# Experts in an order found on chip, and two matmul passes for the five smallest of them

## The chip, the cores and the metric

The kernel runs on one core of a Trainium2 chip. The metric is the time of one execution on the device in microseconds (us), taken as the median of several runs. One execution was also recorded by the hardware profiler; rows and traces below come from it. The engines are TensorE (PE, its weight loads PEld), VectorE (DVE), ScalarE (ACT), GpSimd (POOL) and SyncE (SP), which issues the transfers.

## The reference

A trunk of two layers on 256 tokens of 2048 channels, all f32. The first layer mixes (pooling and attention) and has a dense SwiGLU; the second mixes by spatial gating and has eight SwiGLU experts, of which each token uses two. Only the experts are touched:

```python
logits = jnp.dot(xt, w_router)                       # 256 x 8
top_vals, top_idx = lax.top_k(logits, 2)
top_w = jax.nn.softmax(top_vals, axis=-1)
gates = jnp.sum(one_hot(top_idx, 8) * top_w[..., None], axis=1)
for e in range(8):                                   # w_gu[e]: 2048 x 2816, w_down[e]: 1408 x 2048
    y = y + gates[:, e:e + 1] * swiglu(xt, w_gu[e], w_down[e])
h = layer_norm(alpha * h + y)
```

On the given inputs the router sends 42, 47, 57, 114, 53, 34, 109 and 56 tokens to experts 0 to 7.

## The kernel before

Every f32 operand of a large matmul is split in two parts: a rounded head and a remainder. A product takes three passes on TensorE: activation head by weight remainder, activation remainder by weight head, head by head (`mm3`, L115 to L119). A weight tile comes by one transfer into one of 5 `raw` buffers (L106), ScalarE casts the head `wh` from it (L107) and VectorE subtracts the remainder `wl` (L108); 4 buffers hold heads and 4 hold remainders. A tile has 4 chunks of 128 rows by 512 columns (1 MB) or less. The framework gives each engine its instructions in an order of its own, worked out ahead; an engine then works through its list in that order and waits on semaphores.

After the router, `top2` gives the choice of each token, and `pos1` gives each token its place, from 1 on, in each expert's list. An expert works on 128 slots. `gather` builds one-hot matrices (L819) that pick the tokens of two experts, multiplies the tokens' heads and remainders by them (L837, two experts side by side, 256 columns) and copies the result to SBUF as `xe` (L839). `slots` builds the transposed one-hot `DT` and the gate of each slot `gs`. `expert_up` does gate and up in three column blocks of 512, 512 and 384, each 16 chunks deep, and SwiGLU after each block (L527, L528, transposes L181, split L174 and L175). `expert_down` does four column blocks, 11 chunks deep; each ends in a scatter: head `yh` (L896) and remainder `yl` (L897) of the gated result, two matmuls by `DT` for each half of the tokens (L900, L901), and an add to `h` (L234). The experts run in the order 0 to 7. The pair's gather for experts 2 and 3 is done in steps within the down stage of expert 1, and so on. The first expert's first block is special: `lead` steps through gather, tokens' parts and loads.

After the last expert come the last LayerNorm (`final_norm`) and a test on the largest count, `most`: an If (L729) holds a loop that would handle tokens beyond 128 of an expert. The experts' loads all go through SP's queue, in order.

Of the kernel before, what the change touches and what calls it, by code (L numbers as in the profile page):

```python
# [10 lines left out]
F32 = mybir.dt.float32  # L11
F32R = mybir.dt.float32r
BF16 = mybir.dt.bfloat16
I32 = mybir.dt.int32
# [18 lines left out]
HALF = 2  # L33
RSQRT_MAGIC = float(0x5F3759DF)
# [7 lines left out]
C_MAIN = 520  # L42
# [7 lines left out]
def make_consts():  # L50
# [9 lines left out]
    c[:, C_IOTA8:C_IOTA8 + NEXP] = np.arange(NEXP)[None, :] - NEXP  # L60
    pos = np.arange(2 * P)
# [11 lines left out]
class Trunk:  # L73
# [23 lines left out]
    def load(self, src, w=CB):  # L97
# [8 lines left out]
        nc.sync.dma_start(raw, src)  # L106
# [532 lines left out]
    def moe(self, pm, stats, G, B):  # L639
# [3 lines left out]
        gall = pm.tile([P, 3, P], F32R, tag="gg", name="gg", bufs=1)  # L643
        nc.vector.tensor_copy(gall[:, 0, :], self.ident)
# [40 lines left out]
        gat = self.gather(xtok, [pos1[t][:, 0:2] for t in range(NT)], gg, 0, 0)  # L685
# [16 lines left out]
        first = lead()  # L702
        for t in range(NT):
            gv = gg[t][:, 1, :2 * NEXP].rearrange("p (e s) -> p e s", s=2)
            nc.scalar.copy(gv[:, :, 0], gates[t])
            nc.vector.tensor_tensor(gv[:, :, 1], gates[t], gv[:, :, 0].bitcast(F32), ALU.subtract)
# [100 lines left out]
    def gather(self, xtok, pos, gg, e, offset, num=2):  # L807
# [36 lines left out]
        def slots():  # L844
            for p in range(num):
                ps = self.ps()
                for t in range(NT):
                    mm(ps[:, t * 256:(t + 1) * 256], Dt[t][:, p, :], gg[t], start=t == 0, stop=True,
                       skip_group_check=True)
                DT = pm.tile([P, NT, P], F32R, tag="DT", name="DT", bufs=3)  # L850
                pv = ps.rearrange("p (a b) -> p a b", a=2)
                nc.scalar.copy(DT, pv[:, :, 0:P])
                gs = pm.tile([P, 1], F32, tag="gs", name="gs", bufs=4)
                nc.vector.tensor_reduce(gs, pv[:, :, P + 2 * (e + p):P + 2 * (e + p) + 2], AX.XY, ALU.add)
                DTs.append(DT)
                gss.append(gs)
        return xe, DTs, gss, quarter, slots

    def expert_up(self, e, gat, p, first=None):
        i, pm = self.i, self.pm  # L860
# [6 lines left out]
        for b, w in enumerate(EXP_W):  # L867
            accs = []
            for u in range(2):
# [4 lines left out]
                groups = self.loads(i["odd_moe_gu"][e, b * 2 + u] if b < 2 else i["odd_moe_gu2"][e, u], w)  # L874
                accs.append(self.block(groups, lhs, 0, w))
            hT.append(self.swiglu(pm, accs[0], accs[1], w, w // P, "m"))
        return hT

    def expert_down(self, e, gat, p, hT, first, stats, step=None):
# [3 lines left out]
        def lhs(k, t):  # L883
            return hT[k // 4][0][:, k % 4, :], hT[k // 4][1][:, k % 4, :]
        for n in range(NCB):
            if step is not None:
                step(n)
            groups = []
            for k in range(0, EXP_KC, PIECE):
                o, kc = k * CB * P, min(PIECE, EXP_KC - k)  # L890
                src = i["odd_moe_down"][e, n][o:o + kc * CB * P].rearrange("(p m) -> p m", p=P)
                groups.append(self.load(src))
            acc = self.block(groups, lhs, 0)
            yh = pm.tile([P, CB], F32R, tag="yh", name="yh", bufs=1)
            yl = pm.tile([P, CB], F32R, tag="yl", name="yl", bufs=1)
# [138 lines left out]
```

## Time and profile before

| what | us |
|---|---|
| runs of the kernel, median (lowest to highest) | 2174.91 (2174.14 to 2175.73) |
| profiled execution, its own time | 2175.96 |
| profiled execution, span of its instructions | 2174.2 |

The span is from the first to the last instruction in the trace; 1.8 us of the profiled time lie around it. Starts in the rows count from the start of the span.

### The profile page before, as it was taken

The page shows a single profiled execution, that of the slowest core. Times are in us where ns is not written, and L with a number is a line of the kernel's source. Part 1 is how long each engine was busy: PE and PEld are TensorE (multiplying, and loading weights), DVE is VectorE, ACT ScalarE, POOL GpSimd, SP SyncE. Part 2 cuts the span into 40 slices and gives each one's busy share as a digit, 9 for nine tenths or more (in the row PEclk, how much of TensorE's full clock was granted, in tenths as well). Part 3 has the DMA queues.
Part 4 walks back from the last instruction along what each step waited for, and adds up shares of the span by engine and source line. Part 5 has one row for each costly group of instructions (what it writes and reads, how often), then busy time and mean ns, then how long its engine had stood idle before and what let it go on. Part 6 is the DMA issues. An engine that isn't in the chain of part 4 may idle for free.

```text
span 2174.2 us, 24450 instructions
## 1 busy us (share of the span) xinstructions
PE 2140.0 (98%) x9955; PEld 1781.5 (82%) x9956; DVE 1456.7 (67%) x1225; ACT 1146.6 (53%) x962; POOL 1.6 (0%) x6
## 2 busy tenths in 40 slices
PE   9999999999999999999999999999999999999996
PEld 7888888888888888888788887888888888888884
DVE  5443566554454644556676546898889888888988
ACT  5444355343333433343644335766766767676764
POOL 0000000000000000000000000000000000000000
PEclk9999999999999999999999999999999999999998
DMA  8544645555454554545544643899989999998995
GB/s 347 217 147 145 233 180 208 211 194 191 157 215 172 213 189 169 204 169 218 213 182 166 235 155 117 320 352 357 340 331 367 347 336 342 346 352 322 371 351 213
DMA packets 82198, 537.80 MB, mean 247 GB/s; under 512 B 9504, under 2 KB 10656, under 8 KB 28192
## 3 DMA queue, kind: packets, MB, share of 16 engines
q1 hardware_dynamic: 82080, 536.18, 66.3%
q8 instruction: 80, 1.31, 0.2%
q14 instruction: 38, 0.31, 0.0%
HBM read 534.04 MB, written 2.10 MB: 247 GB/s over the span
## 4 chain that ended last, share of the span: by engine, by line
PE 93%; DVE 3%; ACT 2%; DMA 1%; issue 0%; SPq 0%; DVEq 0%; ACTq 0%
PE acc L118 29%; PE acc L119 28%; PE acc L117 28%; PE ps L181 2%; DVE wl L108 1%; PE ps L837 1%; ACT wh L107 1%; PE ps L900 1%; DMA raw<-in_odd_moe_down_dram 1%; DMA raw<-in_even_w_in_dram 1%; PE ps L901 1%; ACT lnT L259 0%; PE ps L575 0%; PE acc L135 0%; PE acc L629 0%
## 5 line engine op out<-in xcount | busy, mean ns | idle before, releaser
L108 DVE TENSOR_TENSOR wl<-raw,wh 128x2048 fp32r<-128x2048 f32 (+2 forms) x519 | 1121.3, 2178 | 391.5 <-ACT wh L107 390.8
L107 ACT CAST wh<-raw 128x2048 fp32r<-128x2048 f32 (+2 forms) x519 | 935.4, 1824 | 442.1 <-PE acc L119 399.3
L118 PE MATMUL acc<-wl,xh 128*128 128x512 f32 x928 | 363.3, 392 | 1.1 <-DVE wl L108 1.1
L117 PE MATMUL acc<-wh,xh 128*128 128x512 f32 x928 | 361.8, 390 | 0.1
L119 PE MATMUL acc<-wh,xl 128*128 128x512 f32 x928 | 361.6, 390 | 0.0
L118 PE MATMUL acc<-wl,xe 128*128 128x512 f32 (+1 forms) x752 | 280.7, 373 | 0.1
L119 PE MATMUL acc<-wh,xe 128*128 128x512 f32 (+1 forms) x752 | 279.4, 372 | 0.0
L117 PE MATMUL acc<-wh,xe 128*128 128x512 f32 (+1 forms) x752 | 278.6, 371 | 0.5 <-ACT wh L107 0.5
L118 PE MATMUL acc<-wl,hTh 128*128 128x512 f32 x704 | 277.3, 394 | 1.1 <-DVE wl L108 1.0
L119 PE MATMUL acc<-wh,hTl 128*128 128x512 f32 x704 | 276.1, 392 | 0.0
L117 PE MATMUL acc<-wh,hTh 128*128 128x512 f32 x704 | 274.8, 391 | 0.0
L118 PEld LDWEIGHTS acc<-wl,xh 128*128 128x128 f32 x928 | 174.4, 188 | 37.0 <-DVE wl L108 1.5
L117 PEld LDWEIGHTS acc<-wh,xh 128*128 128x128 f32 x928 | 174.2, 188 | 37.1 <-ACT xh L174 0.5
L119 PEld LDWEIGHTS acc<-wh,xl 128*128 128x128 f32 x928 | 174.4, 188 | 35.7 <-DVE xl L175 0.2
L118 PEld LDWEIGHTS acc<-wl,xe 128*128 128x128 f32 x752 | 141.2, 188 | 21.2 <-DVE wl L108 1.8
L117 PEld LDWEIGHTS acc<-wh,xe 128*128 128x128 f32 x752 | 141.2, 188 | 20.7 <-ACT wh L107 0.8
L118 PEld LDWEIGHTS acc<-wl,hTh 128*128 128x128 f32 x704 | 132.3, 188 | 30.3 <-DVE wl L108 3.5
L119 PEld LDWEIGHTS acc<-wh,xe 128*128 128x128 f32 x752 | 141.3, 188 | 19.0
L117 PEld LDWEIGHTS acc<-wh,hTh 128*128 128x128 f32 x704 | 132.3, 188 | 28.3
L119 PEld LDWEIGHTS acc<-wh,hTl 128*128 128x128 f32 x704 | 132.4, 188 | 26.4
L174 ACT CAST hTh<-ps 128x512 fp32r<-128x512 f32 (+1 forms) x46 | 26.2, 569 | 180.4 <-PE ps L181 180.4
L117 PE MATMUL acc<-wh,x0h 128*128 128x512 f32 x256 | 104.1, 409 | 2.5 <-ACT wh L107 2.5
(201 smaller groups left out, 1820.0 us busy)
## 6 DMA issues: line engine op xcount, KB each, us to landing
raw<-in_odd_moe_gu_dram SPq DMA_DIRECT2D x128, 1024.0 KB, 6.9
raw<-in_even_ffn_gu_dram SPq DMA_DIRECT2D x88, 1024.0 KB, 4.8
raw<-in_odd_moe_down_dram SPq DMA_DIRECT2D x64, 1024.0 KB, 7.0
raw<-in_odd_moe_gu_dram SPq DMA_DIRECT2D x64, 768.0 KB, 6.1
raw<-in_even_ffn_down_dram SPq DMA_DIRECT2D x44, 1024.0 KB, 4.8
raw<-in_odd_w_in_dram SPq DMA_DIRECT2D x32, 1024.0 KB, 4.8
raw<-in_even_w_in_dram SPq DMA_DIRECT2D x30, 1024.0 KB, 5.0
raw<-in_odd_moe_down_dram SPq DMA_DIRECT2D x32, 768.0 KB, 6.8
```

The costliest lines, as they stand in the source:

```text
L107: nc.scalar.copy(wh, raw)
L108: self.wl_ins = nc.vector.tensor_tensor(wl, raw, wh.bitcast(F32), ALU.subtract)
L117: mm(acc, xh, wh, start=first, stop=False)
L118: mm(acc, xh, wl, start=False, stop=False)
L119: mm(acc, xl, wh, start=False, stop=last)
L174: self.nc.scalar.copy(hi, src)
L181: self.nc.tensor.transpose(ps[:, j * P:(j + 1) * P], src[:, j * P:(j + 1) * P], self.ident)
L837: mm(o, xtok[t, c // 8][part][:, cs], Dt[t].rearrange("p a b -> p (a b)"), start=j == 0 and t == 0, stop=t == 1, skip_group_check=True)
L900: nc.tensor.matmul(ps, DT[:, t, :], yh, start=True, stop=False)
L901: nc.tensor.matmul(ps, DT[:, t, :], yl, start=False, stop=True)
```

## The change

An expert with at most 64 tokens needs only 64 slots. The change puts head and remainder of its 64 tokens side by side as the 128 columns of one stationary operand, so that a pass by `wh` and a pass by `wl` give all four products; the two halves of the result are then added by one more matmul by a shifted identity (`fold`) after a copy by ScalarE. Gate and up, and down, are done that way (`two`, `slim_expert`); in down the halves are added by the scatter's matmul, since the one-hots name each slot twice.

Which experts are that small is known only on chip. Expert 0 runs first, as before. During it `order` computes for the seven others a permutation: those with over 64 tokens first; SP reads the seven indices into registers, and the loads take their addresses from these. The first two in that order always run in three passes. For the last five an If on the number of experts over 64 (`full`) chooses: if it is at most two, the five run by `slim_expert`; else all run in three passes. Two loads of the first of the five are traced ahead of the If. The gathers are now of one expert (the first), of two, and within the If's first arm of two and of three; the arm's second gather is done in steps in the down stage of its second expert. The dispatch gates and positions are permuted by the same matrix. Loads, casts and remainders of the weights stay as they are. `down_loads`, `scatter` and `slots` hold lines that stood in `expert_down` and `gather` before.

```diff
+SLIM = 64
+EARLY = 2
+FATS = 2
+REST = NEXP - 1
...
-        nc.sync.dma_start(raw, src)
+        self.issued = nc.sync.dma_start(raw, src)
...
+        self.fold = pm.tile([P, P], F32R, tag="fold", name="fold", bufs=1)
+        nc.gpsimd.memset(self.fold[:, SLIM:].bitcast(F32), 0.0)
+        nc.gpsimd.tensor_copy(self.fold[:, :SLIM], self.ident[:, SLIM:])
...
-        gat = self.gather(xtok, [pos1[t][:, 0:2] for t in range(NT)], gg, 0, 0)
+        gat = self.gather(xtok, [pos1[t][:, 0:1] for t in range(NT)], gg, 0, 0, num=1)
...
+        def gate_cols(t, gates, at, num):
+            gv = gg[t][:, 1, at:at + 2 * num].rearrange("p (e s) -> p e s", s=2)
+            nc.scalar.copy(gv[:, :, 0], gates)
+            nc.vector.tensor_tensor(gv[:, :, 1], gates, gv[:, :, 0].bitcast(F32), ALU.subtract)
...
-        for e in range(NEXP):
-            cur = gat
-            hT = self.expert_up(e, cur, e % 2, None if e else first)
-            if e == 0:
+        many = pm.tile([P, REST], F32, tag="many", name="many", bufs=1)
+        nc.vector.tensor_scalar(many, cnt[:, 1:NEXP], float(SLIM), None, ALU.is_gt)
+        ids, posP, full = [], [], pm.tile([P, 1], I32, tag="full", name="full", bufs=1)
+
+        def gather(k, num):
+            return self.gather(xtok, [posP[t][:, k:k + num] for t in range(NT)], gg, NEXP + k, 0, num=num)
+
+        def gather_slim(k, num):
+            return self.gather_slim(xtok, [posP[t][:, k:k + num] for t in range(NT)], num)
+
+        def prepare():
+            order = self.order(many, pos1, gates, gate_cols, posP, full)
+            ins, v = nc.values_load_multi_w_load_instructions(
+                order[0:1, :], engines=[mybir.EngineType.SP], min_val=1, max_val=REST)
+            self.after(ins[0], self.issued)
+            ids.extend(v)
+        hT = self.expert_up(0, gat, 0, first, prepare)
+        gat[4]()
+        cur, gat = gat, gather(0, FATS)
+        gat[4]()
+        self.expert_down(0, cur, 0, hT, True, None, gat[3])
+        for p in range(FATS):
+            hT = self.expert_up(ids[p], gat, p)
+            self.expert_down(ids[p], gat, p, hT, False, None)
+        full_v = nc.values_load(full[0:1, 0:1], min_val=0, max_val=REST)
+        src = i["odd_moe_gu"][ids[FATS], 0]
+        early = [self.load(src[k]) for k in range(EARLY)]
+        with tc.If(full_v < FATS + 1) as slim:
+            at = 0
+            A, step = gather_slim(FATS, 2)
+            for q in range(4):
+                step(q)
+            for k in range(FATS, REST):
+                ahead = partial(gather_slim, k + 1, REST - k - 1) if k == FATS + 1 else None
+                nxt = self.slim_expert(ids[k], k - FATS - at, A, gg, NEXP + k, fstats if k == REST - 1 else None,
+                                       early if k == FATS else None, ahead)
+                if nxt is not None:
+                    A, at = nxt, 2
+        with slim.Else():
+            for k in range(FATS, REST, 2):
+                num = min(2, REST - k)
+                gat = gather(k, num)
                 gat[4]()
-            step = None
-            if e % 2 and e + 1 < NEXP:
-                gat = self.gather(xtok, [pos1[t][:, e + 1:e + 3] for t in range(NT)], gg, e + 1, 0)
-                gat[4]()
-                step = gat[3]
-            self.expert_down(e, cur, e % 2, hT, e == 0, fstats if e == NEXP - 1 else None, step)
+                for q in range(4):
+                    gat[3](q)
+                for p in range(num):
+                    hT = self.expert_up(ids[k + p], gat, p, early=None if k + p > FATS else early)
+                    self.expert_down(ids[k + p], gat, p, hT, False, fstats if k + p == REST - 1 else None)
 
...
+    def order(self, hv, pos1, gates, gate_cols, posP, full):
...
+        e7 = self.c[:, C_IOTA7:C_IOTA7 + R]
+        rank, a, b = (tile(f"ord{k}", [P, R]) for k in range(3))
+        H = tile("ordH", [P, 1])
+        ids = tile("ids", [P, R], I32)
+        sq, perm = tile("ordsq", [P, R, R]), tile("perm", [P, R, R])
+        self.after(v.tensor_reduce(H, hv, AX.X, ALU.add), self.wl_ins)
+        v.tensor_copy(full, H)
+        v.tensor_tensor(sq, rows(hv), square(C_LOWER), ALU.mult)
+        v.tensor_reduce(rank, sq, AX.X, ALU.add)
+        v.scalar_tensor_tensor(a, e7, H, rank, ALU.add, ALU.subtract)
+        v.tensor_tensor(b, rank, a, ALU.subtract)
+        v.tensor_tensor(b, b, hv, ALU.mult)
+        v.tensor_tensor(a, a, b, ALU.add)
+        v.tensor_tensor(perm, rows(a), square(C_PLACE), ALU.is_equal)
+        v.tensor_scalar(b, e7, 1.0, None, ALU.add)
+        v.tensor_tensor(sq, perm, rows(b), ALU.mult)
+        v.tensor_reduce(b, sq, AX.X, ALU.add)
+        v.tensor_copy(ids, b)
+        for t in range(NT):
+            g = tile("gateP", [P, R], bufs=2)
+            x = tile("posP", [P, R], bufs=2)
+            for dst, src in ((x, pos1[t]), (g, gates[t])):
+                v.tensor_tensor(sq, perm, rows(src[:, 1:NEXP]), ALU.mult)
+                v.tensor_reduce(dst, sq, AX.X, ALU.add)
+            gate_cols(t, g, 2 * NEXP, R)
+            posP.append(x)
+        return ids
...
+    def gather_slim(self, xtok, pos, num):
...
+        slots = self.iota1[:, :SLIM].unsqueeze(1).to_broadcast([P, 2, SLIM])
+        d4 = []
+        for t in range(NT):
+            d = pm.tile([P, num, 2, SLIM], F32R, tag="Dt", name="d4", bufs=2)
+            for p in range(num):
+                nc.vector.tensor_scalar(d[:, p], slots, pos[t][:, p:p + 1], None, ALU.is_equal)
...
+        A, units = {}, {}
+        per = 4 // num if num < 3 else 1
+        w = num * SLIM
+        hold = 8 // num if num < 3 else 2
+
+        def quarter(q):
+            for c in range(4 * q, 4 * q + 4, per):
+                if c % hold == 0:
+                    units[0] = self.unit("xs", shape=[P, hold, num, 2, SLIM])
+                ps = self.ps()
+                for j in range(per):
+                    cs = slice((c + j) % 8 * P, ((c + j) % 8 + 1) * P)
+                    for part in range(2):
+                        o = ps[:, (2 * j + part) * w:(2 * j + part + 1) * w]
+                        for t in range(NT):
+                            mm(o, xtok[t, (c + j) // 8][part][:, cs], d4[t][:, :, 0, :],
+                               start=j == 0 and part == 0 and t == 0, stop=t == 1, skip_group_check=True)
+                for j in range(per):
+                    u = units[0][:, (c + j) % hold]
+                    nc.scalar.copy(u, ps[:, 2 * j * w:2 * (j + 1) * w].rearrange("p (a e s) -> p e a s", a=2, e=num))
+                    A[c + j] = u
+        return (A, d4), quarter
...
+    def slim_expert(self, e, p, gat, gg, col, stats, early, ahead):
...
+        A, d4 = gat
+
+        def two(groups, lhs, w):
+            acc = self.acc()
+            n, k0 = sum(g[2] for g in groups), 0
+            for wh, wl, kc in groups:
+                for j in range(kc):
+                    mm(acc[:, :w], lhs(k0 + j), wh[:, j, :], start=k0 + j == 0, stop=False)
+                    mm(acc[:, :w], lhs(k0 + j), wl[:, j, :], start=False, stop=k0 + j == n - 1)
+                k0 += kc
+            return acc
+
+        def fold(acc, w):
+            c = self.pln.tile([P, CB], F32R, tag="lnT", name="low")
+            nc.scalar.copy(c[:, :w], acc[:, :w])
+            mm(acc[:, :w], self.fold, c[:, :w], start=False, stop=True, skip_group_check=True)
+
+        hT = []
+        for b, w in enumerate(EXP_W):
+            accs = [two(self.up_loads(e, b, u, early),
+                        lambda k: A[k][:, p], w) for u in range(2)]
+            for acc in accs:
+                fold(acc, w)
+            nch = w // P
+            s = self.pln.tile([P, CB], F32, tag="lnT", name="silu")
+            nc.scalar.activation(s[:, :w], accs[0][:, :w], AF.Silu)
+            nc.vector.tensor_tensor(s[:, :w], s[:, :w], accs[1][:, :w], ALU.mult)
+            pv = self.transpose4(s, nch)[:, :w].rearrange("p (c t) -> p c t", c=nch)[:, :, :SLIM]
+            h = pm.tile([P, 4, 2, SLIM], F32R, tag="hTh", name="hT2", bufs=3)
+            nc.scalar.copy(h[:, :nch, 0, :], pv)
+            nc.vector.tensor_tensor(h[:, :nch, 1, :], pv, h[:, :nch, 0, :].bitcast(F32), ALU.subtract)
+            hT.append(h)
+        DT, gs = self.slots([d4[t][:, p] for t in range(NT)], gg, col)
+        nxt, step = (None, None) if ahead is None else ahead()
+        for n in range(NCB):
+            if step is not None:
+                step(n)
+            acc = two(self.down_loads(e, n), lambda k: hT[k // 4][:, k % 4], CB)
+            self.scatter(acc, DT, gs, n, False, stats)
+        return nxt
...
+                accs.append(self.block(self.up_loads(e, b, u, early), lhs, 0, w))
             hT.append(self.swiglu(pm, accs[0], accs[1], w, w // P, "m"))
+            if then is not None and b == 0:
+                then()
...
```

## Rows read from the trace of the kernel before

**Rows 1.** The page's first part: busy us, share, instructions.

```profile
PE 2140.0 (98%) x9955; PEld 1781.5 (82%) x9956; DVE 1456.7 (67%) x1225; ACT 1146.6 (53%) x962; POOL 1.6 (0%) x6
```

**Rows 2.** Windows: us, busy PE, PEld, DVE, ACT, POOL (count), PEclk, DMA share, GB/s.

```profile
900.00:1000.00 100.00, 100.00 (x447) 82.38 (x446) 50.27 (x32) 39.92 (x26) 0.00 (x0) 1.00 0.47 173
1454.85:1559.06 104.21, 104.19 (x516) 89.26 (x515) 87.53 (x62) 77.43 (x66) 0.00 (x0) 1.00 0.93 348
1559.06:1654.54 95.48, 95.48 (x448) 81.45 (x447) 83.80 (x54) 65.38 (x46) 0.00 (x0) 1.00 0.92 345
2055.34:2152.68 97.34, 96.48 (x447) 80.85 (x445) 85.30 (x59) 63.34 (x45) 0.00 (x0) 1.00 0.87 330
1454.85:2152.68 697.83, 696.03 (x3333) 592.84 (x3331) 598.82 (x397) 492.54 (x375) 0.00 (x0) 1.00 0.92 344
```

**Rows 3.** Waits, 1400 to 2100: us in total, times, longest; then SP's queue.

```profile
ACT wh L107 <- PE acc L119: 36.8, 48, 1.3
...
DVE silu L528 <- PE acc L119: 19.4, 17, 2.0
...
ACT wh L107 <- DMA raw<-in_odd_moe_down_dram: 9.3, 12, 1.4
...
SPq L106 <- DVE wl L108: 595.0, 252, 5.2
```

**Rows 4.** Windows where the DMA share is 1.00, columns as in rows 2.

```profile
20.00:50.00 30.00, 29.79 (x131) 24.35 (x131) 16.84 (x11) 15.13 (x14) 0.00 (x0) 1.00 1.00 410
1368.00:1390.00 22.00, 22.00 (x100) 18.19 (x100) 20.65 (x12) 15.79 (x10) 0.00 (x0) 1.00 1.01 392
1430.00:1450.00 20.00, 20.00 (x89) 16.48 (x89) 19.59 (x15) 14.49 (x11) 0.00 (x0) 1.00 1.00 365
```

**Rows 5.** Groups by line and shape from 1340 on: busy us, mean ns.

```profile
L839 ACT CAST xe<-ps 128x512 fp32r<-128x512 f32 x64 | 34.7, 592 | 13.4 <-PE ps L837 13.3
...
L819 DVE TENSOR_SCALAR Dt<-c,pos 128x128 fp32r<-128x128 f32 x16 | 3.5, 282 | 0.0
```

**Rows 6.** Lines L728, L729: ns min/median/max, first and last start.

```profile
L728 SPq TENSOR_LOAD <-most x1: 472/472/472, 1347.6 to 1347.6; - x1
...
L728 SPq FUSED_REGOPS  x1: 179/179/179, 1348.1 to 1348.1; - x1
...
L729 PEldq COMPARE_BRANCH  x1: 3370/3370/3370, 2155.0 to 2155.0; - x1
...
L729 DVEq COMPARE_BRANCH  x1: 72/72/72, 2169.0 to 2169.0; - x1
```

**Rows 7.** Timelines by engine: start, us, instruction, idle before.

```profile
1343.52 0.16 DVE L789 TENSOR_REDUCE idx<-eq 128x1 f32<-128x8 f32 x1
...
1364.80 13.30 DVE L108 TENSOR_TENSOR wl<-raw,wh 128x2048 fp32r<-128x2048 f32 x6
...
1376.46 1.92 ACT L107 CAST wh<-raw 128x2048 fp32r<-128x2048 f32 x1 [0.80 <-PE acc L119]
...
1422.86 0.66 ACT L852 CAST DT<-ps 128x256 fp32r<-128x256 f32 x2
...
1306.54 1.06 PE L629 MATMUL acc<-gR,rT 128*128 128x8 f32 x8
...
1359.41 1.10 PE L837 MATMUL ps<-Dt,xth 128*128 128x256 f32 x8
```

**Rows 8.** The page's sixth part: issues, KB each, median us to landing.

```profile
raw<-in_odd_moe_gu_dram SPq DMA_DIRECT2D x128, 1024.0 KB, 6.9
```

**Rows 9.** Timelines of the tail, ScalarE, then VectorE.

```profile
2152.68 0.69 ACT L896 ACTIVATE yh<-acc,gs 128x512 fp32r<-128x512 f32 x1 [7.84 <-PE acc L119]
...
2154.74 1.28 DVE L234 TENSOR_TENSOR h<-h,ps 128x512 f32<-128x512 f32 x2 [0.59 <-PE ps L901]
```

**Rows 10.** TensorE's timeline and a window, columns as in rows 2.

```profile
1347.03 2.05 PE L837 MATMUL ps<-Dt,xth 128*128 128x256 f32 x8 [1.94 <-DVE Dt L819]
...
1345.20:1348.60 3.40, 1.57 (x7) 1.61 (x8) 3.40 (x17) 0.84 (x3) 0.00 (x0) 0.50 0.00 0
```

More of the change, by code (lines that the diff above doesn't have):

```diff
@@ L845, in slots @@
             for p in range(num):
[L846 to L854, printed above, removed]
+                DT, gs = self.slots([Dt[t][:, p, :] for t in range(NT)], gg, e + p)
                 DTs.append(DT)
@@ L857, in gather, with slots @@
         return xe, DTs, gss, quarter, slots
-    def expert_up(self, e, gat, p, first=None):
-        i, pm = self.i, self.pm
+    def slots(self, d, gg, col):
+        nc, pm = self.nc, self.pm
+        ps = self.ps()
+        for t in range(NT):
+            nc.tensor.matmul(ps[:, t * 256:(t + 1) * 256], d[t], gg[t], start=t == 0, stop=True,
+                             skip_group_check=True)
+        DT = pm.tile([P, NT, P], F32R, tag="DT", name="DT", bufs=3)
+        pv = ps.rearrange("p (a b) -> p a b", a=2)
+        nc.scalar.copy(DT, pv[:, :, 0:P])
+        gs = pm.tile([P, 1], F32, tag="gs", name="gs", bufs=4)
+        nc.vector.tensor_reduce(gs, pv[:, :, P + 2 * col:P + 2 * col + 2], AX.XY, ALU.add)
+        return DT, gs
@@ L861, in expert_up @@
+    def expert_up(self, e, gat, p, first=None, then=None, early=None):
+        pm = self.pm
         xe = gat[0]
@@ L887, in expert_down, with up_loads, down_loads, scatter @@
                 step(n)
[L888 to L895, printed above, removed]
-            nc.scalar.mul(yh, acc, gs)
-            nc.vector.scalar_tensor_tensor(yl, acc, gs, yh.bitcast(F32), ALU.mult, ALU.subtract)
-            for t in range(NT):
-                ps = self.ps()
-                nc.tensor.matmul(ps, DT[:, t, :], yh, start=True, stop=False)
-                nc.tensor.matmul(ps, DT[:, t, :], yl, start=False, stop=True)
-                self.add_stats(t, n, ps, None if stats is None else stats[t], first)
+            acc = self.block(self.down_loads(e, n), lhs, 0)
+            self.scatter(acc, DT, gs, n, first, stats)
+    def up_loads(self, e, b, u, early):
+        i = self.i
+        src = i["odd_moe_gu"][e, b * 2 + u] if b < 2 else i["odd_moe_gu2"][e, u]
+        if early is None or b or u:
+            return self.loads(src, EXP_W[b])
+        return early + [self.load(src[k]) for k in range(EARLY, src.shape[0])]
+    def down_loads(self, e, n):
+        groups = []
+        for k in range(0, EXP_KC, PIECE):
+            o, kc = k * CB * P, min(PIECE, EXP_KC - k)
+            src = self.i["odd_moe_down"][e, n][o:o + kc * CB * P].rearrange("(p m) -> p m", p=P)
+            groups.append(self.load(src))
+        return groups
+    def scatter(self, acc, DT, gs, n, first, stats):
+        nc, pm = self.nc, self.pm
+        yh = pm.tile([P, CB], F32R, tag="yh", name="yh", bufs=1)
+        yl = pm.tile([P, CB], F32R, tag="yl", name="yl", bufs=1)
+        nc.scalar.mul(yh, acc, gs)
+        nc.vector.scalar_tensor_tensor(yl, acc, gs, yh.bitcast(F32), ALU.mult, ALU.subtract)
+        for t in range(NT):
+            ps = self.ps()
+            nc.tensor.matmul(ps, DT[:, t, :], yh, start=True, stop=False)
+            nc.tensor.matmul(ps, DT[:, t, :], yl, start=False, stop=True)
+            self.add_stats(t, n, ps, None if stats is None else stats[t], first)
     def load_consts(self):
```

31 lines of the change are left out of this document (25 added, 6 removed).

## Prediction

> **What bounds the kernel now.** I read the busy shares first. TensorE is busy 98% of the span [rows 1], so its work counts first. The change touches the eight experts alone, so I went to the stretches between the start of the last `yh` (L896) of one expert and that of the next. Seven of them make 697.8 us, the experts 1 to 7. An expert without a gather in its stretch takes 95.5 us, one with the next pair's gather 104.2, and TensorE is busy all through both [rows 2]. Its work explains the length: the dense stretch of the FFN gives 447 matmuls in 100 us, 0.224 us for 512 columns [rows 2]; an expert has 324 of 512 columns and 96 of 384, with 16 more for the scatter, so 324 x 0.224 + 96 x 0.168 + 16 x 0.224 = 92.3 us and a few transposes.
>
> What is next behind TensorE? In the same 95.5 us VectorE is busy 83.8 us, mostly in the 36 remainders of L108, and the DMA engines' share is 0.92 [rows 2]. In the waits of the expert stage the casts (L107) wait for TensorE to give back a `wh` buffer for 36.8 us and for a transfer of the down weights 9.3 us, and the queue that issues loads waits 595 us for VectorE to free a `raw` buffer [rows 3]. So loads are held back by TensorE, through buffers, with two other resources close behind. That is the point of the whole forecast: what is taken off TensorE is worth only what these two let through.
>
> Bytes: an expert has 2048 x 2816 + 1408 x 2048 f32 weights, 34.6 MB in 36 loads, 0.961 MB a load. Where the DMA share is 1.00, the trace shows 410 GB/s early in the kernel, 392 while the first expert refills its buffers, and 365 where VectorE is busy 98% as well [rows 4]. A load at these rates takes 2.34, 2.45 and 2.63 us. VectorE needs 83.8 / 36 = 2.33 us per load if it never waits.
>
> **Which arm runs.** The reference's router sends 42, 47, 57, 114, 53, 34, 109 and 56 tokens to the experts. Two of the last seven exceed 64, so `full` is 2, the condition `full < 3` holds, the two fat ones come first and the five others take two passes.
>
> **The change, part by part.**
>
> *Two passes instead of three, five times.* Per expert 64 + 44 matmuls of 512 columns and 32 of 384 go: 108 x 0.224 + 32 x 0.168 = 29.6 us, 148 us in all. Added per expert: six folds, 1.3 us. TensorE needs some 68 us per slim expert with its share of the gathers; loads take 36 x 2.34 to 36 x 2.63, 84 to 95 us. So the arm runs at the pace of the loads. I take 2.5 us a load, between the 392 and the 365 row, because VectorE and the transfers are nearly level there and five `raw` buffers tie them together; bounds 2.34 and 2.63. The loads' casts and remainders themselves stay as they are. ScalarE gains six fold copies (0.6 us each by the like of L839 [rows 5]) and stays under 75 us.
>
> *Small things.* The constants grow by 54 KB (0.13 us at 410 GB/s), and GpSimd builds the fold matrix while it has nothing else: 0.
>
> *Dynamic addresses.* A few register operations more per load on SP; one bundle of them took 0.18 us [rows 6]. The 595 us of waiting on that queue hide it; without that cover it were 252 x 0.18 = 45 us.
>
> *Order on chip.* `order` is 27 small VectorE instructions, some 0.2 us apart by the like of L789 [rows 7], 5 us, behind the remainder of load 7. VectorE works without a pause until 1378.1 there; TensorE gave back load 4's buffer at 1376.4 [rows 7] and has three more loads of 12 x 0.224 = 2.7 us, until 1384.5; the next remainder comes at 1385.6 instead of 1380.6: +1 us. Then SP loads seven registers; one load took 0.47 us and 0.18 of checks [rows 6], so 0.7 to 4.6 us. Behind it on SP stand the loads of the first expert's second block, and TensorE waits for them; the buffers already filled cover 10 us. If the instruction stands ahead of load 8 and waits for `ids`, transfers stop about 7 us and the chain landing (6.9 us [rows 8]), cast, remainder leaves TensorE idle some 8 us. I take +1, bounds 0 and +8; the like load for `most` stood on SP at 1347.6, where its data was ready [rows 6], not at the end of the program.
>
> *Gathers.* The first becomes one of a single expert: 16 copies of 128x256 instead of 128x512, 0.33 for 0.59 us [rows 5, 7], 4.2 us of ScalarE, of which I count half since others overlap: -2 (0 to -4). TensorE gains nothing: 8 matmuls of 8 columns take 1.06 us, 8 of 256 take 1.10 [rows 7], so narrow ones cost the same; eight follow each other at some 0.117. The pair's gather moves into the first expert's down stage, +8.7 us as before (104.2 - 95.5). The gathers of two and three stand in the arm; the second is hidden, since TensorE has slack there.
>
> *Entry of the arm.* Nothing of the arm can run ahead of the branch. From the second fat expert's last matmul: `yh`, `yl`, scatter and two adds, 3.4 us by the tail [rows 9]; register load 0.5 and branch 0.07 on VectorE [rows 6]; four one-hots of 0.28 [rows 5]: 5.1 us. The gather is 64 x 0.117 = 7.5 us; with its last copy and the handoff (0.7) TensorE begins the arm's loads at 13.3. Its first load (8 matmuls, 1.8 us) frees a `wh`, a cast and a remainder (1.9 + 2.2) free a `raw`, and with the handoffs transfers resume at 19.5. By then 9 of the arm's 180 loads are in: two issued early, two more, five in `raw`. TensorE's pause may bring the low clock: around a pause of 1.9 us the granted clock was 0.50, that is 1.2 GHz, from 1345.2 on [rows 10], and the gather would cost 7.5 more.
>
> So the arm takes 19.5 + 171 x 2.5 + 7 (landing, cast, remainder, last matmuls of the last load) = 454 us.
>
> *Exit of the arm.* VectorE jumps over the other arm before the last LayerNorm. VectorE's near branch took 0.07 us, TensorE's, over 500 matmuls, 3.37 us [rows 6]. VectorE's jump crosses some 280 instructions; I take +3.4, bounds 0.07 and 3.4. The Trainium skill ("Runtime: NRT & Kernel Launch", Instruction fetch mechanics) says that prefetch is sequential and that a taken branch out of the fetched pages waits for a fetch; the trace agrees for TensorE's 3.37 us, and by that rule VectorE pays alike. SP waits for its transfers and jumps as well, before `load_gb`; G and B are needed some 10 us after the last load landed, so this stays hidden.
>
> **The sum.** In place of the 697.8 us stand 8.7 (pair gather) + 2 x 95.5 + 454, plus 2 for the last expert's statistics (97.3 against 95.5 [rows 2]): 655.7, or -42.1. With -2, +1 and +3.4: -39.7. The profiled execution took 2175.96 us (span 2174.2 and 1.8 around it), so 2136.3; the median shown is 1.05 lower: 2135.
>
> **The rivals.**
>
> *Transfers stay at their contended rate* (2.63 us a load): 171 x 0.13 = +22, 2157. For it: the 365 row is from this very stage. Against: 392 a little earlier. The Trainium skill ("DMA: Bandwidth & Descriptors", Specifications) gives about 358 GB/s per core as the HBM limit; the trace's 410 over 30 us disagrees. By that limit a load is 2.68 us and the time 2166, an estimate from that page.
>
> *No contention at all* (2.34): 171 x 0.16 = -27, 2108. For it: VectorE's 2.33 us is possible, and 410 was reached. Against: two resources at 100% through five buffers.
>
> *Slower: the fold's chain.* Each of 15 up blocks ends in copy, fold, copy, fold, SiLU, then VectorE's product; with a cast (1.9 us) ahead of each copy on ScalarE that is 4 to 5 us. If VectorE's order puts the product before remainders that are ready, VectorE, now the pace, stands still that long: 15 x 4.5 = 68 us, 2203. It decides from 39.7 / 15 = 2.6 us a block. For it: VectorE already waits 19.4 us, 17 times, for TensorE at L528 [rows 3]. Against: the longest of these is 2.0 us, and four buffers of remainders stand between.
>
> *Slower: the clock.* TensorE would pause about 0.7 us after every load in the arm. If it were granted 0.50 for over 60% of the arm, its 340 us of work would fill the time saved; all at 0.50 it were 2 x 340 = 680, 226 more than 454, 2361. Against: at half clock it would be busy without pauses again, and where it is so the clock stands at 1.00 [rows 2].
>
> *The other arm runs.* All seven keep three passes; the entry's 13 us, one jump of 3.4 and a fifth gather of 7.5 come on top, less 1: 2198. Against: the counts, the third largest being 57.
>
> **Chances.** Likeliest case 0.57 (own range 2115 to 2156: order, jump, clock at entry and half the spread of a load); contended rate 0.20, of which 0.03 near no change, with a slow entry on top; no contention 0.10; fold 0.08; clock 0.03; other arm 0.02. Taking about 0.2% as what a measurement tells from no change: faster 0.84, the same 0.03, slower 0.13. The range goes from 2106 to 2170; it leaves out the three slower cases and the edges of the others.
>
> **What would show it.** After the fat experts the stretches of L896 should be 86 to 95 us long, TensorE some 75% busy, VectorE above 90%, and the casts should wait for transfers, no longer for TensorE. At the entry TensorE should stand still twice, some 5 us before the gather. Two `expert_up` stretches of 95.5 should remain. On VectorE a branch of about 3.4 us should stand before L204. I am wrong if VectorE waits long at the SiLU product in the arm, if the load's pace there is over 2.7 us, or if TensorE's clock falls between loads.

## The result

The change makes the kernel slower: 2243.46 us (2240.53 to 2244.87), before 2175.32 in the same comparison, a ratio of 1.0312 (1.0294 to 1.033). The forecast was 2135. The first view is the windows between the starts of the last `yh` (L1098 now) of one expert and the next: full experts 1 and 2, then the five slim experts (the first holds the arm's entry and the pair's gather, the second the gather of three), then the tail.

```profile
core 0: us, PE busy (x) PEld busy (x) DVE busy (x) ACT busy (x) POOL busy (x), PEclk, DMA share, GB/s
1462.53:1558.78 96.25, 96.25 (x448) 81.49 (x447) 84.51 (x54) 66.22 (x46) 0.00 (x0) 1.00 0.93 345
1558.78:1655.97 97.19, 96.82 (x447) 81.07 (x445) 85.17 (x55) 66.79 (x46) 0.00 (x0) 1.00 0.96 356
1655.97:1777.43 121.46, 93.04 (x380) 69.62 (x380) 85.15 (x59) 75.50 (x69) 0.00 (x0) 0.93 0.78 286
1777.43:1893.16 115.73, 85.90 (x380) 62.73 (x381) 86.95 (x62) 77.96 (x71) 0.00 (x0) 1.00 0.83 300
1893.16:1998.43 105.27, 77.36 (x315) 54.15 (x314) 85.27 (x55) 70.83 (x55) 0.00 (x0) 1.00 0.89 329
1998.43:2105.09 106.66, 79.37 (x315) 54.42 (x315) 85.35 (x56) 70.87 (x55) 0.00 (x0) 1.00 0.88 325
2105.09:2214.26 109.17, 80.77 (x314) 55.39 (x314) 86.48 (x61) 67.05 (x52) 0.00 (x0) 0.98 0.81 293
2214.26:2238.80 24.54, 1.47 (x4) 0.59 (x4) 15.99 (x43) 5.02 (x7) 0.00 (x0) 0.62 0.26 91
```

Up to 1655.97 all goes as forecast (1653.6 by its terms); the tail is 24.5 us for 21.5. The loss is in the arm: 2214.26 - 1655.97 = 558.3 us, forecast 454. A slim expert without a gather takes 105 to 109 us, though no engine is busy for more than 86.5 of them and the DMA share is lower than before the change [rows 2]. So no single engine's work accounts for the length; waits do. Here are those of 1777 to 2214 (who waits, for whom, us in total, times, longest):

```profile
PEld acc L1012 <- DVE wl L119: 147.7, 134, 2.9
ACT wh L118 <- PE acc L1011: 114.6, 106, 2.6
PE acc L1012 <- DVE wl L119: 97.3, 104, 2.4
DVE wl L119 <- ACT wh L118: 81.5, 82, 2.6
```

TensorE waits for VectorE's remainder, VectorE for ScalarE's cast, and the cast for TensorE: a circle. Before, the casts waited 36.8 us for TensorE in a longer stretch (1400 to 2100) [rows 3], and TensorE's weight loads 4.2 us for a remainder:

```profile
PEld acc L118 <- DVE wl L108: 4.2, 9, 0.8
```

The timeline of the changed kernel shows one turn (start, duration, in brackets the idle time before and what ended it):

```profile
1693.33 1.91 ACT L118 CAST wh<-raw 128x2048 fp32r<-128x2048 f32 x1 [2.07 <-PE acc L1011]
1695.27 4.49 DVE L119 TENSOR_TENSOR wl<-raw,wh 128x2048 fp32r<-128x2048 f32 x2 [1.51 <-ACT wh L118]
1695.53 1.90 ACT L118 CAST wh<-raw 128x2048 fp32r<-128x2048 f32 x1 [0.29 <-PE acc L1011]
...
1697.62 0.50 PE L1012 MATMUL acc<-wl,xs 128*128 128x512 f32 x1 [1.66 <-DVE wl L119]
...
1699.11 0.39 PE L1011 MATMUL acc<-wh,xs 128*128 128x512 f32 x1
...
1699.54 1.91 ACT L118 CAST wh<-raw 128x2048 fp32r<-128x2048 f32 x1 [1.13 <-PE acc L1011]
```

The cast at 1693.33, its remainder (2.25, ready at 1697.5), TensorE from its first product with `wl` (1697.62) to the last one with `wh` (1699.50), and then the next cast into that buffer: 6.2 us, in which two loads pass. With four buffers four should. Where the other two buffers are is seen at the arm's entry: TensorE has used up both early loads with the product at 1679.14, yet the next cast starts only when the last product with the third load's `wh` (1680.73) is done, and VectorE has stood still for 10.8 us. The DMA engines are idle from 1678 to 1686.

```profile
1679.14 0.39 PE L1012 MATMUL acc<-wl,xs 128*128 128x512 f32 x1
...
1680.73 0.39 PE L1011 MATMUL acc<-wh,xs 128*128 128x512 f32 x1
...
1681.16 3.71 ACT L118 CAST wh<-raw 128x2048 fp32r<-128x2048 f32 x2 [6.18 <-PE acc L1011]
...
1683.10 4.49 DVE L119 TENSOR_TENSOR wl<-raw,wh 128x2048 fp32r<-128x2048 f32 x2 [10.83 <-ACT wh L118]
```

```profile
1680.00:1685.00 5.00, 3.62 (x15) 2.46 (x14) 1.90 (x1) 3.84 (x3) 0.00 (x0) 1.00 0.00 0
```

The buffer addresses in the built program agree: ahead of the branch `wh` and `wl` turn through four addresses each, and all 178 loads of the arm through two. **Theory A**: `early` is allocated outside the branch, so its `wh` and `wl`, which are read inside, keep their buffers until the whole arm is over. Rivals: **B**, the branch itself costs; **C**, two passes with a fold must wait for the remainder at each load.

### The profile page after: what moved, and what is told of

The parts are those of the page before. It is cut to its first block, busy times and chain, and to the rows that moved or that the text cites. A ratio compares the mean times of both kernels' runs of the same rounds, so it can differ in the third digit from the quotient of the medians.

```text
span 2238.8 us, 23731 instructions
## 1 busy us (share of the span) xinstructions
PE 2061.8 (92%) x9286; PEld 1654.4 (74%) x9286; DVE 1461.9 (65%) x1249; ACT 1157.7 (52%) x994; POOL 1.9 (0%) x8
## 4 chain that ended last, share of the span: by engine, by line
PE 79%; DVE 11%; ACT 7%; issue 1%; DMA 1%; SPq 0%; DVEq 0%; ACTq 0%
PE acc L129 22%; PE acc L130 22%; PE acc L128 21%; DVE wl L119 9%; ACT wh L118 7%; PE acc L1012 4%; PE acc L1011 3%; PE ps L192 2%; PE ps L991 1%; PE ps L893 1%; PE ps L1103 1%; PE acc L146 0%; PE acc L139 0%; PE ps L1102 0%; PE acc L145 0%
## 5 line engine op out<-in xcount | busy, mean ns | idle before, releaser
L1012 PE MATMUL acc<-wl,xs 128*128 128x512 f32 (+1 forms) x480 | 192.2, 401 | 84.1 <-DVE wl L119 83.3
L1012 PEld LDWEIGHTS acc<-wl,xs 128*128 128x128 f32 x480 | 90.5, 189 | 136.1 <-DVE wl L119 125.5
L130 PE MATMUL acc<-wh,hTl 128*128 128x512 f32 x484 | 190.3, 393 | 0.0
L129 PE MATMUL acc<-wl,hTh 128*128 128x512 f32 x484 | 189.8, 392 | 0.3 <-DVE wl L119 0.3
L128 PE MATMUL acc<-wh,hTh 128*128 128x512 f32 x484 | 189.3, 391 | 0.0
L1011 PE MATMUL acc<-wh,xs 128*128 128x512 f32 (+1 forms) x480 | 182.1, 379 | 3.5 <-ACT wh L118 3.3
L1012 PE MATMUL acc<-wl,hT 128*128 128x512 f32 x220 | 92.7, 421 | 34.0 <-DVE wl L119 34.0
L1011 PEld LDWEIGHTS acc<-wh,xs 128*128 128x128 f32 x480 | 91.0, 190 | 17.2 <-ACT wh L118 6.4
L129 PE MATMUL acc<-wl,x0h 128*128 128x512 f32 x256 | 101.5, 397 | 0.4 <-DVE wl L119 0.4
L130 PE MATMUL acc<-wh,xe 128*128 128x512 f32 (+1 forms) x272 | 101.0, 372 | 0.0
```

Of the source, the lines that this page charges most:

```text
L128: mm(acc, xh, wh, start=first, stop=False)
L129: mm(acc, xh, wl, start=False, stop=False)
L130: mm(acc, xl, wh, start=False, stop=last)
L1011: mm(acc[:, :w], lhs(k0 + j), wh[:, j, :], start=k0 + j == 0, stop=False)
L1012: mm(acc[:, :w], lhs(k0 + j), wl[:, j, :], start=False, stop=k0 + j == n - 1)
```

## The experiments

Times are medians, ratios against the kernel before, with their 95% intervals.

**What holds the loop.** Four edits of the changed kernel: no load ahead of the branch; one; no branch and both loads; the other arm.

```
early0:   EARLY = 2  ->  EARLY = 0
early1:   EARLY = 2  ->  EARLY = 1
no_if:    - with tc.If(full_v < FATS + 1) as slim:   (body kept, Else left out)
else_arm: - tc.If(full_v < FATS + 1)   + tc.If(full_v < 1)
```

> The two loads issued ahead of the branch are moved into the arm (EARLY = 0); nothing else changes. Theory A (tiles made ahead of the branch keep their buffers until the whole arm is over, so only two of the four wh/wl pairs turn there: cast 1.90 + remainder 2.29 + some 1.8 of TensorE = 6.0 us for each two loads, 3.0 a load): four pairs turn again, 6.0/4 = 1.5 us is no limit, and the arm goes at the pace of VectorE (85 us busy per expert) or of the transfers (33.2 MB per expert at 350 GB/s = 95 us): 86 to 95 us per slim expert in place of 105 to 116, time 2140 to 2180. The loads are hidden behind the pair gather anyway. Theory B (the branch itself, its entry and exit, is what costs): 2235 to 2255, since the branch is still there. Theory C (two passes with a fold are bound to wait for the remainder at each load): 2240 or more, pace unchanged.

> One load ahead of the branch in place of two (EARLY = 1). Theory A: three pairs of buffers turn, 6.0/3 = 2.0 us a load, under what VectorE needs for a load (85/36 = 2.4), so nearly all of the loss is gone: 2140 to 2185, within 10 us of the run with none ahead; a loss that falls only by half (about 2205) would say that the count of buffers matters in another way. Theories B and C: 2235 to 2255.

> The branch and its other arm are left out (the two-pass arm always runs; that is the arm taken for these inputs, so the general case alone is lost); both loads are still issued ahead. Theory A: without a branch the buffers of the two early loads come free when they are used, four pairs turn: 86 to 95 us per slim expert and 2130 to 2180; a few us under the run with EARLY = 0 (the jump at the end of the arm, 3.0). Theory B: the same time as theory A here, but then EARLY = 0 alone must not help. Theory C: 2235 to 2245.

> The branch is kept with both early loads, but its condition is changed so that the other arm runs (three products in full width, no fold, pair gathers). Theory A: that arm has two buffer pairs too, and TensorE holds each for longer (11 products of 0.235 = 2.6 us from the first remainder product to the last use): 1.9 + 2.3 + 2.6 = 6.8 us for two loads, 3.4 a load, some 115 to 122 us per expert: 2285 to 2330, slower than the changed kernel. Theory C: the three-product arm goes as the experts before it, 96 to 99 us per expert: about 2195 to 2205.

Measured: early0 2185.22 us (1.005; 1.0033 to 1.0067), early1 2189.66 (1.0068; 1.0051 to 1.0085), no_if 2170.96 (0.9979; 0.997 to 0.9989), else_arm 2339.4 (1.0757; 1.0739 to 1.0775). Theory A holds: 58 us come back by an edit of one constant with the branch in place, and three pairs are within 4.4 us of four. In the other arm experts 2 and 4 take 122.2 us, 122.2 / 36 = 3.39 a load where 3.4 was worked out, and C falls by early0 and by this arm, which has no fold; the total is 9 us over my range, since the stretches with a gather take 137 to 141. The second expert of that arm:

```profile
1793.71:1915.93 122.22, 104.06 (x447) 79.02 (x446) 86.69 (x55) 68.83 (x46) 0.00 (x0) 1.00 0.80 283
```

B is left with 14.3 us (early0 against no_if): 9.1 in the first slim expert (108.9 and 99.8, first row early0, second no_if), where nothing of the arm runs ahead of the branch, and 3.1 in the tail (24.7 and 21.6).

```profile
1655.14:1764.05 108.91, 90.84 (x380) 69.81 (x380) 85.98 (x60) 75.19 (x71) 0.00 (x0) 0.92 0.82 305
1656.50:1756.31 99.81, 86.13 (x380) 67.15 (x380) 81.45 (x55) 72.46 (x69) 0.00 (x0) 0.95 0.89 334
```

That is for this order of products; the order of wh_first without the branch was not run. But early0 and early1 miss theory A's range by some 5 us, and no_if, where all four pairs turn, still needs 491.8 us for the arm. Something else binds there.

**The circle made longer, and cut.** One load more held, and TensorE's share of the circle taken out with both loads held, by the order of the products (within a load all with `wh` first, then all with `wl`):

```
early3:   EARLY = 2  ->  EARLY = 3
wh_first:
      for j in range(kc):
          mm(acc[:, :w], lhs(k0 + j), wh[:, j, :], start=k0 + j == 0, stop=False)
  +   for j in range(kc):
          mm(acc[:, :w], lhs(k0 + j), wl[:, j, :], start=False, stop=k0 + j == n - 1)
wh_first_early1: the same, EARLY = 1
```

> Three early loads, so by theory A one pair of buffers is left: each load must go through cast, remainder and TensorE before the next one's cast: 6.0 us for a load of 1 MB, some 4.9 for one of 0.75 MB, mean 5.6; 172 loads and the entry give some 980 us for the arm where the changed kernel has 558: 2620 to 2740 in all. If held buffers weren't the cause, one more load ahead would leave the time at 2235 to 2250.

> The changed kernel with its branch and both early loads; only the order of TensorE's products within a load changes in the two-pass arm: the four with wh first, then the four with wl. Theory A says what the held buffers cost is a circle through both: cast 1.90, remainder 2.29, then TensorE alternating from the first wl product to the last wh product 1.8. With wh first TensorE uses wh while the remainder is made, so wh turns in 1.9 + 2.3 = 4.2 us for two loads and wl in 2.3 + 1 = 3.3: 2.1 and 1.7 a load, both under VectorE's 2.4. So most of the 58 us should come back with two buffers still held: 2170 to 2195. If the number of buffers decides whatever the order (latency of the transfers, say), it stays at 2235 to 2245.

> The same order with one early load in place of two: three pairs turn. With the circle gone already, the third pair adds slack only: 2165 to 2190, at or a few us under the run with two early loads; the transfers (theory D) bound both.

Measured: early3 2910.39 us (1.3383; 1.3356 to 1.341), wh_first 2177.94 (1.0013; 1.0003 to 1.0022), wh_first_early1 2170.06 (0.9977; 0.9967 to 0.9986). So 65.5 us are gone with two buffers still held: it is the circle through them that costs, not their number alone. In the windows the arm takes 491.8 us:

```profile
1654.81:2146.56 491.75, 409.04 (x1703) 292.05 (x1703) 424.19 (x290) 358.13 (x296) 0.00 (x0) 0.99 0.91 347
```

early3 is beyond my range by 170 us, in A's direction. Its timeline shows why:

```profile
2002.79 1.90 ACT L118 CAST wh<-raw 128x2048 fp32r<-128x2048 f32 x1 [5.34 <-PE acc L1011]
2004.72 2.29 DVE L119 TENSOR_TENSOR wl<-raw,wh 128x2048 fp32r<-128x2048 f32 x1 [4.95 <-ACT wh L118]
...
2007.07 0.79 PE L1012 MATMUL acc<-wl,xs 128*128 128x512 f32 x1 [1.83 <-DVE wl L119]
...
2010.03 1.90 ACT L118 CAST wh<-raw 128x2048 fp32r<-128x2048 f32 x1 [5.34 <-PE acc L1011]
```

One load in 7.24 us. Cast and remainder are the 4.3 us that I used; TensorE takes 2.96 us instead of 1.8 from its first product with `wl` to the end of the last with `wh`, at one product in 0.43 us where the changed kernel's turn had one in 0.23. The granted clock is lower as well (0.60):

```profile
1900.00:2000.00 100.00, 57.09 (x119) 33.88 (x118) 35.06 (x19) 29.48 (x20) 0.00 (x0) 0.60 0.40 140
```

**What binds when the circle is cut.** **Theory D**: the transfers. **Theory E**: ScalarE's queue, in which casts stand behind the copy for the fold; in no_if that copy (L1006 there) waits 61.8 us for TensorE. The first two below are no_if with about half of the bytes of the slim experts (it computes with other weights) and without the fold (the two halves are not added); the third is no_if with the other arm's body; the fourth has the pair's gather in the second full expert; the last is the kernel before with about half of the bytes of its last five experts.

```
half_bytes, before_half (last five experts):
  + r = 2 if kc == 4 else 1
  + dma_start(raw[:, :r], src[:, :r])
  + rb = raw[:, :r].unsqueeze(1).to_broadcast([P, kc // r, r, w])   # cast and subtraction read rb
no_fold:     - for acc in accs: fold(acc, w)
no_if_three: the body of Else in place of that of If
lead_static: + A, step = gather_slim(FATS, 2)   for p == FATS - 1, step into expert_down
```

> The branch-free kernel (2170.96 us) with about half of the weight bytes of the five slim experts left out: each of their loads fetches two of its four rows (one of three) and the cast and the subtraction read those rows twice (three times), so that every engine does the work it did and only the transfers shrink; the output is that of other weights. Theory D (with four buffers back, the transfers bound the arm: share 0.96 at 352 to 370 GB/s in its stretches): the arm goes at VectorE's pace, 80 to 89 us per expert in place of 87 to 104, about 20 to 45 us less: 2125 to 2150. Theory E (the casts stand in ScalarE's queue behind the copy for the fold, which waits 61.8 us in 24 places for the end of a block): unchanged, 2163 to 2175.

> The branch-free kernel with the fold left out (the copy of the sums on ScalarE and the product that adds the lower half; the SiLU reads the unfolded sums, so part of the computation is missing). Theory E: ScalarE no longer waits at the copy, but it waits for the same block end at the SiLU one step on, so perhaps half of the 61.8 us of waits comes back: 2140 to 2160. Theory D: the transfers go on at 350 to 370 GB/s, 2165 to 2174.

> No branch, and the last five experts with three products as before (the other arm, always): what is left of the change is the order worked out on chip, the addresses from registers, and the gathers moved. By the terms of the prediction this is the time before with the order and the startup (+1 - 2) and no other difference: 2172 to 2180. Against the branch-free two-pass kernel (2170.96) it gives what two passes are worth: by the prediction's 2.5 us a load in place of 2.7 some 30 to 40 us (2200 to 2210 here), by theory D, with the transfers the limit of both, 0 to 10 us.

> The branch-free kernel with the first pair's gather moved out of the arm's entry: it is issued in quarters ahead of the down blocks of the second full expert, as the pair gathers were before. In the entry the transfers stand at a share of 0.27 for 10 us and TensorE runs at a granted clock of 0.64 there. If the entry's pause costs what it shows, some 8 to 12 us go: 2158 to 2164. If the transfers merely catch up afterwards, the gather adds its 8 to 9 us of TensorE to a stretch where TensorE has no gap: 2168 to 2175.

> The kernel before with about half of the weight bytes of its last five experts left out (rows fetched once and read twice; the output is that of other weights), its three products unchanged. Theory D: before stood on TensorE (busy 696 of 698 us) with the transfers close behind at a share of 0.93, so fewer bytes give nothing: 2170 to 2177; the two-pass arm by contrast got 37 us from the same edit. If the transfers were the limit before as well, 2130 to 2150.

Measured: half_bytes 2134.07 us (0.9802; 0.9786 to 0.9818), no_fold 2171.82 (0.998; 0.997 to 0.999), no_if_three 2207.44 (1.0143; 1.0126 to 1.016), lead_static 2168.09 (0.9966; 0.9952 to 0.9981), before_half 2175.38 (1.0001; 0.9992 to 1.0011). E falls: without the copy and its product the time stays, and though the SiLU then waits for TensorE in its place, for 34.9 us, half_bytes keeps the copy and yet gains 37 us. For D: fewer bytes give the two-pass arm those 37 us and the kernel before nothing. The third and fourth slim experts, first in no_if, then in half_bytes:

```profile
1859.62:1946.47 86.85, 73.92 (x316) 54.81 (x314) 80.03 (x54) 65.68 (x52) 0.00 (x0) 1.00 0.96 370
1946.47:2044.38 97.91, 77.99 (x316) 55.92 (x315) 84.35 (x56) 68.81 (x53) 0.00 (x0) 0.98 0.96 352
```

```profile
1849.56:1935.51 85.95, 76.39 (x316) 57.28 (x314) 80.49 (x54) 69.55 (x55) 0.00 (x0) 0.96 0.60 189
1935.51:2024.11 88.60, 77.32 (x315) 57.41 (x315) 83.42 (x56) 69.83 (x55) 0.00 (x0) 0.96 0.60 190
```

With the bytes halved VectorE is busy for 80 to 83 of 86 to 89 us and comes nearest to setting the pace. The whole arm, no_if and half_bytes:

```profile
1656.50:2148.34 491.84, 403.22 (x1703) 299.01 (x1703) 422.49 (x286) 353.35 (x296) 0.00 (x0) 0.98 0.92 347
```
```profile
1656.15:2114.14 457.99, 404.46 (x1703) 307.70 (x1703) 419.30 (x286) 356.41 (x296) 0.00 (x0) 0.95 0.58 183
```

no_if_three splits what I had put down. I had expected 30 to 40 us between three and two passes, and D 0 to 10: 36.5 were found. But the three-pass kernel isn't at 2172 to 2180, where the prediction's own terms and D would have it: it is 32 us over the kernel before (2207.44 against 2175.68). Its stretches without a gather are like those before (97.2 and 96.7); those with one take 110.2, 110.3 and 112.2 where before had 104.9, 104.3 and 97.3 (the last without a gather):

```profile
1657.37:1767.61 110.24, 106.70 (x516) 91.27 (x517) 86.98 (x61) 77.64 (x65) 0.00 (x0) 0.98 0.85 319
2071.81:2184.02 112.21, 109.58 (x513) 93.10 (x513) 86.39 (x60) 71.07 (x62) 0.00 (x0) 0.95 0.77 284
```

There the gathers stand at the start of a pair instead of between down blocks, and there are five of them instead of four; what each costs was not separated. So two passes are worth 36 us in this arrangement, and with three passes the arrangement costs 32. lead_static, with one gather moved back, is 2.9 us below no_if by the medians, and the intervals of the two overlap: no gain is shown.

**Transfers or staging buffers.** Fewer bytes shorten a transfer and the round trip through `raw` alike. The base is wh_first_early1; the other run drops its early load.

```
raw4:            self.pool("raw", 5)  ->  self.pool("raw", 4)
wh_first_early0: EARLY = 1  ->  EARLY = 0
```

> The kernel with wh first and one early load, with four staging buffers (raw) in place of five. A load's round trip there is 6.9 us from issue to landing, then cast 1.9 and remainder 2.3, some 11.1 us at the least. If the round trip through the staging buffers sets the pace of the slim experts, it goes from 11.1/5 = 2.2 to 11.1/4 = 2.8 us a load, 100 us per expert in place of 88 to 97, and the full experts (96) slow to that too: 2210 to 2260. If the rate of the transfers is the limit (share 0.95 to 0.98), a load lands sooner when fewer are under way, and the time stays within some 10 us: 2168 to 2182.

> The order with wh first and no load ahead of the branch: all four buffer pairs turn, and the entry waits for its first load. Against one early load (2170.06) it tells what the early load is worth once the order no longer needs the buffers: if the pair gather hides the first loads, 2165 to 2172; if the entry shows them, as the 108.9 us of the first slim expert in the run with EARLY = 0 against 107.3 with EARLY = 1, 2172 to 2178.

Measured: raw4 2210.49 us (1.0156; 1.0132 to 1.018), wh_first_early0 2170.31 (0.9977; 0.9968 to 0.9987). The pure rate of the transfers falls: one staging buffer less costs 40 us. A fixed round trip of 11.1 us gave the right sum, 11.1 / 4 = 2.8, for the last three slim experts took 98.3, 100.1 and 105.2 us, 2.8 a load; but its terms don't hold: a load lands sooner with four buffers (first row wh_first_early1, second raw4; least, median, longest over both sizes of load), so that landing, cast and remainder make 10.1 / 4 = 2.5.

```profile
DMA to landing us min/median/max: 4.3/6.9/9.0
```
```profile
DMA to landing us min/median/max: 4.3/5.9/8.3
```

The two are tied together: with five buffers at a DMA share of 0.96 to 0.98, a load's landing probably contains time behind other loads; that was not measured apart. Whether a sixth buffer would help was not tried: the kernel's on-chip memory, as it is laid out, has no room for it. wh_first_early0 equals wh_first_early1 within 0.3 us, so with this order the early loads are worth nothing.

## Why the prediction was wrong

**The step that failed** is in the entry of the arm: "Its first load (8 matmuls, 1.8 us) frees a `wh`, a cast and a remainder (1.9 + 2.2) free a `raw`". The first load was made ahead of the branch, and its `wh` is never freed in the arm; nor is the second's. Transfers were to go on with the tenth load 19.5 us after the last down product, at 1675.4; they were idle from 1678, with nine in, to 1686. And 171 x 2.5 rested on four pairs where two turned, at 6.2 us for two loads. With the circle shortened by the order of products the arm takes 491.8 us instead of 558.3: 66.5 of the 104 us.

**The pace of a load was mis-sized too.** With the circle shortened, the last four slim experts of wh_first_early1 take

```profile
1762.02:1863.38 101.36, 87.89 (x386) 64.83 (x385) 88.30 (x63) 79.71 (x71) 0.00 (x0) 0.98 0.95 359
1863.38:1951.28 87.90, 75.19 (x311) 53.51 (x310) 81.10 (x55) 65.82 (x53) 0.00 (x0) 1.00 0.98 376
1951.28:2046.09 94.81, 77.43 (x316) 54.07 (x315) 84.18 (x56) 68.91 (x54) 0.00 (x0) 1.00 0.97 366
2046.09:2143.18 97.09, 78.57 (x315) 54.18 (x313) 86.61 (x61) 67.31 (x52) 0.00 (x0) 0.99 0.89 337
```

in the mean 95.3 us, 2.65 a load (2.59 without the first of them, which holds the gather of three): near the rival of the contended rate (2.63) and not 2.5. On 171 loads 0.15 us more are 25 us. Halving the bytes gives 34 (491.8 in no_if, 458.0 in half_bytes), where the last four slim experts take 2.72 and 2.49 us a load. 66.5 and 25 to 34 leave 4 to 13 of the 104 us, of which some 5 are the entry below; the rest was not traced. half_bytes, with no branch, no held buffers and about half of the bytes, comes to 2134: what the forecast described is a kernel that it wasn't given. That this agrees with 2135 to 1 us is partly chance, since half_bytes has neither the branch at the entry nor the jump at the exit, which were in the sum. The Trainium skill ("DMA: Bandwidth & Descriptors", Specifications) has some 358 GB/s per core as the HBM limit. The 359 to 376 GB/s of the first three rows are close to it and above, so it is no hard limit here, but it was a better guide to the pace than the 384 GB/s behind my 2.5 us (0.961 MB).

**Entry.** TensorE began the arm's loads at 1674.09, 18.2 us after its last down product ended (1655.9), forecast 13.3. The gather took 13.8 us instead of 7.5: the low clock, which I had named and left out of the sum.

```profile
1660.29 0.78 PE L991 MATMUL ps<-d,xth 128*128 128x128 f32 x2 [1.63 <-DVE d L974]
...
1674.09 0.73 PE L1011 MATMUL acc<-wh,xs 128*128 128x512 f32 x1
```

The stretches at the start of the gather:

```profile
1655.00:1660.00 5.00, 2.40 (x9) 1.01 (x7) 4.41 (x7) 0.69 (x1) 0.00 (x0) 1.00 1.04 385
1660.00:1665.00 5.00, 4.71 (x22) 4.67 (x22) 0.54 (x3) 1.56 (x5) 0.00 (x0) 0.53 0.53 218
1665.00:1670.00 5.00, 5.00 (x25) 5.00 (x25) 2.31 (x2) 4.58 (x7) 0.00 (x0) 0.50 0.16 21
```

The granted clock fell to 0.50, 1.2 GHz, after a stretch in which TensorE was busy for 2.4 of 5 us, and stayed there while it was busy without a pause, up to some 1677, where its products of 512 columns go from one in 0.43 us to one in 0.23.

**Exit.** The tail is 3.0 us longer (forecast 3.4). VectorE stands still for 1.67 us with nothing to wait for, then the last LayerNorm begins:

```profile
2217.53 1.28 DVE L247 BATCH_NORM_STATS2 stats<-h 128x6 f32<-128x512 f32 x2
2220.48 0.26 DVE L215 BATCH_NORM_AGGREGATE mv<-stats 128x2 f32<-128x24 f32 x1 [1.67 <-issue]
```

Before, the same instruction followed the statistics without a pause:

```profile
2157.14 0.38 DVE L204 BATCH_NORM_AGGREGATE mv<-stats 128x2 f32<-128x24 f32 x2
```

It agrees in kind with the Trainium skill's rule ("Runtime: NRT & Kernel Launch", Instruction fetch mechanics) that a taken branch out of the fetched pages waits for a fetch, at half the size I took; the profile names nothing that ended the pause, so a fetch is not shown. That the other 1.3 us come from the order of the instructions behind it was not tested.

**Right:** the last `yh` of the first expert at 1462.53, 7.7 us later than before, which is 8.7 - 2 + 1; two full experts of 96.3 and 97.2 (95.5); TensorE with slack in the arm (busy 73 to 75%); addresses from registers (96.7 and 97.2 us an expert in no_if_three, 95.5 and 96.2 before: 1 us at most). **The rivals:** no contention at all (2.34 us a load) falls with 2.65 measured, and the contended rate was near for the load but stood alone, without the circle; the fold's chain falls (no_fold); the clock as a rival falls too, for it stood at 0.98 to 1.00 in the arm behind the entry; the other arm was not the one that ran, and would have taken 2339, not 2198, since its buffers are held too. The rival that came true, a wait of casts for buffers across a branch, was not among them: I had read that the casts wait for TensorE to give buffers back [rows 3] and took it as something the change relieves.

**Which version.** wh first with one early load keeps the branch and both arms and takes 2170.06 us, 0.23% under the kernel before; with no early load it takes 2170.31, the same. That is all that is left of a forecast 40: before_half shows that the transfers were no limit before, when TensorE was busy for 696.0 of 697.8 us [rows 2], but they stand so close behind it (share 0.92 [rows 2]) that taking work off TensorE uncovers them at once.

## What to carry to other kernels

A tile that is handed into a branch takes its buffer with it: count the buffers that still turn inside, for that is the depth of the pipeline there. Where buffers are few, follow one buffer round its circle (cast, remainder, first to last use) and divide by their number; the order of uses within a load can shorten the circle as well as another buffer does. And before work is taken off an engine, halve the next resource's load in the kernel as it is and in the one to come: the two runs say how far the gain can go.

## What was not expected of the hardware

In early3 TensorE, busy for 60 to 62% of each slim expert, with two pauses of 1.6 and 1.8 us in each 7.2, was granted 0.58 to 0.63 of its clock, which lengthened the circle by 1.2 us; in the changed kernel, busy for 73 to 75%, with one pause of about 2 us in each 6, it kept 0.98 to 1.00 behind the first slim expert. Half of the bytes left the DMA engines at a share of 0.60 (189 GB/s), not at half of 0.96: the number of packets of the whole kernel stayed (82198), those loads came in packets of about half the size, and at 0.60 for 189 GB/s the engines were busy for longer per byte than at 0.96 for 352 to 370.
